# A hybrid encoder trunk on one core: step sizes of the state space mixer in three parts, two copies at high priority, a norm by token tile

## The chip, the cores and the metric

The kernel runs on one core of a Trainium2 chip. Its engines are TensorE (PE), VectorE (DVE), ScalarE (ACT), GpSimd (POOL) and SyncE (SP), which issues nearly all DMAs. The metric is the device time of one execution in microseconds, as a median over runs.

## What is computed

One layer is applied to two independent sequences, a prompt of 256 tokens and a sample of 512, with the same weights and a width of 1024. Together they are 768 tokens, six token tiles of 128.

```python
def trunk(x, ...):
    h = rmsnorm(x, norm1)
    (gq, gk, gv, gg, glr, dq, dk, dvv, sz, sxbc, sdt) = jnp.split(h @ w_in, IN_OFFSETS, axis=-1)
    o_gla  = gla_mixer(gq, gk, gv, gg, glr, ...)         # gated linear attention, 4 heads
    o_diff = diff_mixer(dq, dk, dvv, ...)                # differential attention, 4 heads
    o_ssd  = ssd_mixer(sz, sxbc, sdt, ...)               # state space mixer, 8 heads
    x = x + jnp.concatenate([o_gla, o_diff, o_ssd], axis=-1) @ w_out
    h = rmsnorm(x, norm2)
    return x + jnp.square(jax.nn.relu(h @ w_mlp1)) @ w_mlp2

def ssd_mixer(sz, sxbc, sdt, ...):
    ...
    dt_f = jax.nn.softplus(sdt[..., :8] + dtb_f)         # the step sizes, one row per head
    dt_b = jax.nn.softplus(sdt[..., 8:] + dtb_b)
    la = dt * a_neg                                      # its running sums give all decays
```

Everything is in fp32. A matrix product is made of three matmuls on halves of fp32 (high by high, low by high, high by low), so each large product costs three.

## The kernel before, in words

**Products.** A unit of weights is 1 MB. It comes in two DMAs of 512 KB into the buffers `wr`; ACT casts each to the high half `wh` (L133), DVE subtracts for the low half `wl` (L134). There are two buffers each of `wr`, `wh` and `wl`. `fm_unit` makes outputs with features on the partitions (tiles `fm`), `tm_unit` with tokens on them (tiles `tm`: 48 matmuls of 256 columns for two token tiles), `tok_product` adds products with `w_out` and the second MLP weights to the residual `xres` (tiles `tp`). The three tiles `fm`, `tm` and `tp` share a pool of three PSUM banks with the transposes `xT` of the second norm of the prompt; all else in PSUM (gates, `tms`, `kTp`, `U`, attention products and so on) shares the other five.

**Gated linear attention.** Two head pairs, hp 0 and 1. `gla_gates` computes running sums of the gates for each: a small product `gate` (L275), ACT and DVE work, a scan. `gla_qk` makes q and k with four `fm` tiles, which ACT copies to SBUF (L304). `gla_core` prepares `qst` and `kst` on DVE, transposes `kst` (`kTp`, L358), copies it (ACT, `kT`, L359), makes the states (`U`, L368, then S), and works through seven levels: exponentials, DVE products, PE products `att` (L435), DVE merges into `A` (L436). Then comes the output `gout` (L446, L447). Here core 0 and core 1 mean the passes of `gla_core` for hp 0 and hp 1. The `tm` products of other parts are spread between the small ones of the cores as filling for PE.

**Step sizes.** `ssd_dt` works on 16 rows: ACT and DVE operations on 16x768, a scan into `dpre` (L499), two writes of the running sums to DRAM (`scr`) and one of the totals (`scp`, L511), a read of the totals back to all partitions (`ptb`, L514), their exponential `decs` on ACT (L519), 12 transposes (`tms`, `tmb`) with nine ACT copies (L528, L532) and six small operations `ew`. Its results are first used in the state space mixer, after both cores. In the code it stands ahead of the gates.

**Second norm of the prompt.** After the last product with `w_out` (`tok_product(y_op, ...)`, column half outside, tile inside), `norm_transpose` squares each tile on ACT, scales it on DVE (`xn`, L176), transposes it on PE (`xT`, L183), and evicts it twice (ACT L184, DVE L185) into `h2`. Two token tiles lie side by side in one bank, so there are eight evictions of 256 columns on each engine. The MLP starts when they are done.

**What sets the order.** The code is written per stage; a list scheduler orders each engine's instructions when the kernel is built, by priority and its own model of durations. `tc.high_priority()` raises what is issued inside it; `tc.issue_after` holds an instruction behind another. On the chip every engine then runs its list in that order, and waits on semaphores.

Of the kernel before, what the change touches and what calls it, by code (L numbers as in the profile page):

```python
# [13 lines left out]
AF = mybir.ActivationFunctionType  # L14
# [5 lines left out]
P = 128  # L20
D = 1024
# [3 lines left out]
SEQS = ((0, 2), (2, 6))  # L25
EPS = 1e-6
LAMBDA_INIT = 0.2
N_IN, N_S3, N_T3, N_T2, N_TT, N_CC, N_DL, N_RAW, N_ACC = 12, 6, 6, 4, 8, 5, 7, 2, 3
N_F = 1024
N_S2, N_DN, N_SC = 3, 4, 2  # L30
LEVELS = (64, 32, 16, 8, 4, 2, 1)
# [11 lines left out]
def hybrid_kernel(ctx, tc, io):  # L43
    nc = tc.nc
    mm, act, dve, pool = nc.tensor.matmul, nc.scalar, nc.vector, nc.gpsimd
# [22 lines left out]
    i3 = tag(ctx, "in", N_IN, 776)  # L68
# [4 lines left out]
    t3 = tag(first, "t3", N_T3, 776)  # L73
# [116 lines left out]
    for tiles in ((0,), (1,), (2, 3), (4, 5)):  # L190
        normed = norm_transpose(xt, 0, tiles, hT, lambda x: (x[:, 0:512], x[:, 512:1024], junk), mx, small, rstd1, tiles[0] * P)

    log_ins = []
# [32 lines left out]
    zdt = s3("zdt")  # L226
# [71 lines left out]
    def gla_qk(hp):  # L298
        c0 = hp * P
        q, k = i3("gq"), i3("gk")  # L300

        def keep(dst, scale):
            def consume(ps, ts):
                act.activation(dst[:, ts], ps, AF.Copy, scale=scale)  # L304
            return consume

        w = load_unit(lambda r: [(0, P, w_in[:, r, C_GQ + c0:C_GQ + c0 + P]),
                                 (P, 2 * P, w_in[:, r, C_GK + c0:C_GK + c0 + P])], (KT, 256))
        fm_unit(w, 0, P, keep(q, 0.125), halves_)
        fm_unit(w, P, P, keep(k, 1.0), halves_)  # L310
        return q, k
# [12 lines left out]
        tm_unit(w, gcons)  # L324
        return sg

    def gla_core(pre, qk, v):
        Pf, Pb = pre
        q, k = qk

# [22 lines left out]
        for h in range(2):  # L353
            kT = t3("kT")
            for (a, b) in ((0, 4), (4, 6)):
                ps = mx("kTp")
# [25 lines left out]
                                                 U(c)[64:128, :], op0=ALU.mult, op1=ALU.add)  # L382
            S.append(sv)

        A = [c4("A", n=T) for _ in range(2)]
# [9 lines left out]
        for li, s in enumerate(LEVELS):  # L397
# [31 lines left out]
            for (a, b) in ((0, 4), (4, 6)):  # L429
                for h in range(2):  # L430
                    hs = slice(64 * h, 64 * h + 64)
                    ps = mx("att")
# [8 lines left out]
        for h in range(2):  # L441
            for (a, b) in ((0, 4), (4, 6)):
                ps = mx("gout")
# [32 lines left out]

    def ssd_dt():

        ps_ = slice(96, 112)
        z, t1, u, l = zdt[ps_], t3("dz")[ps_], t3("dt2")[ps_], t3("dl")[ps_]  # L480
        act.activation(t1, z, AF.Abs)
        act.activation(t1, t1, AF.Exp, scale=-1.0)
        act.activation(l, t1, AF.Ln, bias=1.0)
        dve.tensor_scalar(u, t1, 1.0, -1.0, op0=ALU.add, op1=ALU.add)
        dve.tensor_tensor(t1, t1, u, ALU.subtract)
        act.activation(u, l, AF.Exp, scale=-1.0)
        dve.tensor_tensor(t1, t1, u, ALU.mult)
        dve.tensor_tensor(l, l, t1, ALU.add)
        stk = t3("stk")
        pool.memset(stk, 0.0)  # L490
        dve.scalar_tensor_tensor(stk[0:16], z, 0.0, l, op0=ALU.max, op1=ALU.add)
        dtl = t3("dtl", n=W129)
        lv_ = v129(dtl[ps_])
        pool.memset(lv_[:, :, 0:1], 0.0)

        dve.tensor_scalar(lv_[:, :, 1:129], v128(stk[0:16]), sdtc[0:16, 3:4], -128.0, op0=ALU.mult, op1=ALU.max)
        pre = t3("dpre", n=W129)
        pr = v129(pre)[ps_]
        dve.tensor_tensor_scan(pre[ps_], resetm[ps_], dtl[ps_], 0.0, ALU.mult, ALU.add)  # L499
        act.copy(v128(stk[32:48]), pr[:, :, 1:129])  # L500
        act.copy(v128(stk[64:80]), pr[:, :, 0:128])
        tot = bc(pr[:, :, 128:129], [16, NT, P])
        dve.tensor_tensor(v128(stk[96:112]), tot, pr[:, :, 1:129], ALU.subtract)
        stb = t3("stb")
        dve.tensor_tensor(v128(stb[0:16]), tot, pr[:, :, 0:128], ALU.subtract)

        scr = dram.tile([16, T], F32, name="scr")
        scp = dram.tile([16, NT], F32, name="scp")
        nc.sync.dma_start(out=scr[0:8, :].rearrange("h (c i) -> h c i", i=P), in_=pr[0:8, :, 1:129])
        nc.sync.dma_start(out=scr[8:16, :].rearrange("h (c i) -> h c i", i=P), in_=pr[8:16, :, 0:128])  # L510
        nc.sync.dma_start(out=scp, in_=pr[:, :, 128])  # L511

        ptb = const.tile([P, 2, 8, NT], F32, name="ptb")
        nc.sync.dma_start(out=ptb.rearrange("p d h c -> p (d h c)"),  # L514
                            in_=bc(scp.rearrange("h c -> (h c)")[None, :], [P, 16 * NT]))
        decs = const.tile([P, NT, 2, 4], F32, name="decs")
        for g in range(2):
            gs = slice(64 * g, 64 * g + 64)
            act.activation(decs[gs], ptb[gs, :, 4 * g:4 * g + 4, :].rearrange("p d h c -> p c d h"), AF.Exp)  # L519

        tms = const.tile([P, NT, 40], F32, name="tms")
        tmb = const.tile([P, NT, 16], F32, name="tmb")
        for (a, b) in ((0, 4), (4, 6)):
            ps = mx("tms")
            for c in range(a, b):
                nc.tensor.transpose(ps[:, (c - a) * P:(c - a) * P + 112], stk[0:112, c * P:(c + 1) * P], ident[0:112, 0:112])
            for o, r, n in ((0, 0, 16), (16, 32, 8), (24, 72, 8), (32, 96, 8)):
                act.copy(tms[:, a:b, o:o + n], v128(ps)[:, :b - a, r:r + n])  # L528
        ps = mx("tmb")
        for c in range(NT):  # L530
            nc.tensor.transpose(ps[:, 16 * c:16 * c + 16], stb[0:16, c * P:(c + 1) * P], ident[0:16, 0:16])
        act.copy(tmb, ps[:, :96].rearrange("p (c r) -> p c r", c=NT))  # L532
        ew = const.tile([P, NT, 2, 2, 8], F32, name="ew")
        act.activation(ew[:, :, 0, 0, :], tms[:, :, 16:24], AF.Exp)
        act.activation(ew[:, :, 0, 1, :], tmb[:, :, 8:16], AF.Exp)
        act.activation(ew[:, :, 1, 0, :], tms[:, :, 32:40], AF.Exp)
        act.activation(ew[:, :, 1, 1, :], tms[:, :, 24:32], AF.Exp)
        dve.tensor_tensor(ew[:, :, 1, 0, :], ew[:, :, 1, 0, :], tms[:, :, 0:8], ALU.mult)
        dve.tensor_tensor(ew[:, :, 1, 1, :], ew[:, :, 1, 1, :], tms[:, :, 8:16], ALU.mult)
        return scr, decs, tms, ew  # L540

    def ssd_conv(us, xt, bcm):
        def conv(j):
# [310 lines left out]
    w_out = io["w_out"][0].rearrange("(k p) c -> p k c", p=P)  # L854
# [89 lines left out]
    v = gla_v(0)  # L944
# [60 lines left out]
    qg8 = const.tile([P, 1], F32, name="qg8")  # L1005
    dve.tensor_scalar(qg8, col(R_QN), 0.125, None, op0=ALU.mult)

    dt = ssd_dt()
    pre = [gla_gates(hp) for hp in range(2)]

    masks = t2("masks").bitcast(U8)[:, :len(LEVELS) * P].rearrange("p (l i) -> p l i", i=P)
    for a, b in ((0, 4), (4, 7)):
# [34 lines left out]
    dve.tensor_scalar(nlam, nlam, -LAMBDA_INIT, None, op0=ALU.add)  # L1047

    qk = gla_qk(0)
    core = gla_core(pre[0], qk, v)  # L1050
    qk, v = gla_qk(1), gla_v(1)
    sg = gla_gate_out(0)
    gla_out(0, core, sg)
    core = gla_core(pre[1], qk, v)
    sg = gla_gate_out(1)
    gla_out(1, core, sg)

# [4 lines left out]
    dl = tag(second, "dl", N_DL, 512)  # L1062
# [64 lines left out]
    def norm2(tiles, h2, c0, ps_of):  # L1127
        return norm_transpose(xres, 8, tiles, h2, xn_of, ps_of, small2, rstd1, c0)

    prompt, sample = (0, 1), (2, 3, 4, 5)  # L1130
# [9 lines left out]
        load_x(t, xp_)  # L1140
    tok_product(from_column(gla_p, 0), 4, w_out, 0, prompt)
    tok_product(from_column(mix_operands(mixa[0], range(4), u_new, dn), 0), 4, w_out, 4, prompt)
    tok_product(y_op, 4, w_out, 8, prompt)
    h2p = [both_in(hp_)("h2", 256) for _ in range(KT)]
    normed = [z.ins for z in norm2(prompt, h2p, 0, acc)]

    for f in range(0, 4096, N_F):
        mlp(f, N_F, [(h2p, 0, 256, 0)], prompt, u_new, dn, store if f == 4096 - N_F else None, (scaled, normed) if f == 0 else ())
# [53 lines left out]
```

## Time and profile before

| | |
|---|---|
| median of 3 runs | 1186.19 us (1180.62 to 1189.1) |
| profiled execution | 1190.88 us, of which the span of the trace is 1188.8 us |
| mean granted TensorE clock | 0.978 |
| busy: PE / DVE / ACT / POOL | 96% / 65% / 46% / 14% |

A profile is of one execution. A busy share is a mean over stages: up to about 460 us the mixers run, up to about 830 us the products with `w_out`, the rest of the attention and the prompt's MLP, and after that the sample's MLP. Idle time is printed in front of the instruction that ended it, with the instruction or DMA that released it. The granted clock is 1.0 where the throttle let TensorE run at 2.4 GHz, and 0.5 where it ran at 1.2 GHz.

### The profile page before, as it was taken

To read this page: it belongs to the slowest core of one execution; us is meant where nothing else is said; L and a number is where in the kernel's file an instruction comes from. 1 tells how busy PE (TensorE), PEld (TensorE's weight loads), DVE (VectorE), ACT (ScalarE), POOL (GpSimd) and SP (SyncE) were. 2 spreads that over 40 slices of the span, in tenths; PEclk is the share of its full clock that TensorE was granted. 3 is DMA by queue.
4 is the path that set the end of the run, shared out by engine and by line. 5 is a ranking of instruction groups with operands and counts; after the bars stand their busy time and mean duration, and the time that the engine had idled before them with its cause. 6 is when DMAs were issued, how large, how long until landed. Compare 5 with 4: busy or idle time off the path is not lost.

```text
span 1188.8 us, 17623 instructions
## 1 busy us (share of the span) xinstructions
PE 1136.2 (96%) x6788; PEld 999.4 (84%) x6788; DVE 768.7 (65%) x1366; ACT 541.1 (46%) x1037; POOL 162.8 (14%) x207
## 2 busy tenths in 40 slices
PE   7979999999999998899988999999999999999998
PEld 7979899899998887698878897787987788787786
DVE  6558979775479577896786687766544444444443
ACT  7455345256266426665765673435322322322331
POOL 2003324140310262110100002200000000000000
PEclk9989999799999999899999999999999999999999
DMA  6312021143254346245645457642232232232331
GB/s 193 96 39 69 4 63 37 36 155 119 65 172 113 109 149 203 74 142 185 186 131 171 134 164 236 228 150 72 72 106 92 86 106 87 91 107 79 99 106 71
DMA packets 118856, 136.62 MB, mean 115 GB/s; under 512 B 8951, under 2 KB 86901, under 8 KB 118773
## 3 DMA queue, kind: packets, MB, share of 16 engines
q1 hardware_dynamic: 118741, 135.50, 36.7%
q8 instruction: 53, 0.87, 0.3%
q14 instruction: 30, 0.25, 0.1%
q10 hardware_dynamic: 32, 0.01, 0.0%
HBM read 121.80 MB, written 13.68 MB: 114 GB/s over the span
## 4 chain that ended last, share of the span: by engine, by line
PE 41%; DMA 12%; DVE 9%; ACT 6%; issue 2%; POOL 0%; SPq 0%; ACTq 0%; DVEq 0%; POOLq 0%
DMA wr<-in_w_mlp 8%; PE tp L97 7%; PE tp L98 7%; PE tp L99 7%; PE fm L97 5%; PE fm L98 5%; PE fm L99 5%; DVE wl L134 3%; ACT wh L133 3%; DMA wr<-in_w_out 2%; DMA er<-scr 1%; DVE zh L558 1%; DVE xres L877 1%; PE tm L97 1%; PE tm L99 1%
## 5 line engine op out<-in xcount | busy, mean ns | idle before, releaser
L133 ACT CAST wh<-wr 128x1024 fp32r<-128x1024 f32 x186 | 189.2, 1048 | 250.5 <-PE tp L99 128.2
L134 DVE TENSOR_TENSOR wl<-wr,wh 128x1024 fp32r<-128x1024 f32 x186 | 228.8, 1252 | 107.7 <-ACT wh L133 105.8
L99 PE MATMUL tm<-wh,hTl 128*128 128x256 f32 x576 | 169.8, 295 | 0.0
L97 PE MATMUL tm<-wh,hTh 128*128 128x256 f32 x576 | 168.0, 292 | 1.7 <-ACT xp L552 1.6
L98 PE MATMUL tm<-wl,hTh 128*128 128x256 f32 x576 | 168.2, 292 | 0.0
L877 DVE TENSOR_TENSOR xres<-tp,xres 128x512 f32<-128x512 f32 x116 | 77.7, 686 | 98.3 <-PE tp L99 98.0
L97 PEld LDWEIGHTS tm<-wh,hTh 128*128 128x128 f32 x576 | 112.3, 195 | 4.0 <-ACT xp L552 1.8
L98 PEld LDWEIGHTS tm<-wl,hTh 128*128 128x128 f32 x576 | 112.1, 195 | 1.7 <-DVE wl L134 0.2
L99 PEld LDWEIGHTS tm<-wh,hTl 128*128 128x128 f32 x576 | 112.2, 195 | 1.3
L98 PE MATMUL fm<-h2l,wh 128*128 128x512 f32 (+1 forms) x288 | 107.1, 373 | 0.0
L97 PE MATMUL fm<-h2h,wh 128*128 128x512 f32 (+1 forms) x288 | 106.9, 373 | 0.0
L99 PE MATMUL fm<-h2h,wl 128*128 128x512 f32 (+1 forms) x288 | 106.7, 371 | 0.0
L97 PE MATMUL tp<-wh,uh 128*128 128x512 f32 x256 | 101.5, 396 | 0.6
L98 PE MATMUL tp<-wl,uh 128*128 128x512 f32 x256 | 100.5, 392 | 0.0
L99 PE MATMUL tp<-wh,ul 128*128 128x512 f32 x256 | 99.7, 395 | 0.0
L97 PE MATMUL fm<-h,wh 128*128 128x256 f32 x256 | 72.3, 284 | 2.4 <-ACT relu L923 2.1
L98 PE MATMUL fm<-h,wh 128*128 128x256 f32 x256 | 72.2, 283 | 0.0
L99 PE MATMUL fm<-h,wl 128*128 128x256 f32 x256 | 71.5, 283 | 0.6 <-DVE wl L134 0.6
L923 ACT ACTIVATE relu<-fm 128x256 f32<-128x256 f32 (+1 forms) x68 | 31.6, 468 | 70.3 <-PE fm L99 70.3
L97 PEld LDWEIGHTS fm<-h2h,wh 128*128 128x128 f32 x288 | 54.7, 190 | 10.1
L99 PEld LDWEIGHTS fm<-h2h,wl 128*128 128x128 f32 x288 | 54.6, 190 | 10.0
L98 PEld LDWEIGHTS fm<-h2l,wh 128*128 128x128 f32 x288 | 54.7, 190 | 9.9
(323 smaller groups left out, 2499.4 us busy)
## 6 DMA issues: line engine op xcount, KB each, us to landing
wr<-in_w_mlp SPq DMA_DIRECT2D x128, 512.0 KB
wr<-in_w_in SPq DMA_DIRECT2D x30, 512.0 KB
wr<-in_w_out SPq DMA_DIRECT2D x24, 512.0 KB
ar<-scr SPq DMA_DIRECT2D x6, 512.0 KB
er<-scr SPq DMA_DIRECT2D x6, 512.0 KB
x<-in_x_sample SPq DMA_DIRECT2D x4, 512.0 KB
wr<-in_w_in SPq DMA_DIRECT2D x8, 256.0 KB
xres<-in_x_sample SPq DMA_DIRECT2D x4, 512.0 KB
```

Source lines behind the costliest of these rows:

```text
L97: mm(out, lhsT=lh, rhs=rh, start=first, stop=False)
L98: mm(out, lhsT=lh, rhs=rl, start=False, stop=False)
L99: mm(out, lhsT=ll, rhs=rh, start=False, stop=last)
L133: act.copy(hi, raw)
L134: dve.tensor_tensor(lo, raw, rd(hi), ALU.subtract)
L558: dve.scalar_tensor_tensor(zh, xp[:, k:k + 772], half[:, 6 * k + j:6 * k + j + 1], zh, op0=ALU.mult, op1=ALU.add)
L877: dve.tensor_tensor(xres[t][:, cs], ps, xres[t][:, cs], ALU.add)
L923: act.activation(r, ps, AF.Relu)
```

## The change

1. `ssd_dt` becomes a generator in three parts. Part 1 (absolute value, exponential, logarithm) runs after q and k of hp 0, part 2 (the DVE and ACT work, the scan and the three writes to DRAM) after the output of core 0, part 3 (`ptb`, `decs`, transposes, `ew`) within core 1, between its states and its levels. Four tiles move between pools, and one pool grows by a buffer.
2. The copies of q and k out of PSUM are issued at high priority.
3. The last product with `w_out` of the prompt runs tile by tile, and the norm of each tile is issued at high priority as soon as its product is done, 128 columns wide: 16 evictions on each of ACT and DVE instead of eight, and the same 16 transposes.

```diff
-N_IN, N_S3, ... = 12, 6, ...
+N_IN, N_S3, ... = 12, 7, ...
@@ gla_qk
         def keep(dst, scale):
             def consume(ps, ts):
-                act.activation(dst[:, ts], ps, AF.Copy, scale=scale)
+                with tc.high_priority():
+                    act.activation(dst[:, ts], ps, AF.Copy, scale=scale)
@@ gla_core, between the states S and the levels
+        if between is not None:
+            between()
@@ ssd_dt
-        z, t1, u, l = zdt[ps_], t3("dz")[ps_], t3("dt2")[ps_], t3("dl")[ps_]
+        z, t1, l = zdt[ps_], i3("dz")[ps_], i3("dl")[ps_]
         act.activation(t1, z, AF.Abs)
         act.activation(t1, t1, AF.Exp, scale=-1.0)
-        act.activation(l, t1, AF.Ln, bias=1.0)
+        log_ins.append(act.activation(l, t1, AF.Ln, bias=1.0).ins)
+        yield
+        u = t3("dt2")[ps_]
...
         nc.sync.dma_start(out=scp, in_=pr[:, :, 128])
+        yield
 
         ptb = const.tile([P, 2, 8, NT], F32, name="ptb")
...
-        return scr, decs, tms, ew
+        yield scr, decs, tms, ew
@@ main
-    dt = ssd_dt()
     pre = [gla_gates(hp) for hp in range(2)]
+    dt_steps = ssd_dt()
...
     qk = gla_qk(0)
+    next(dt_steps)
+    dt = []
     core = gla_core(pre[0], qk, v)
     qk, v = gla_qk(1), gla_v(1)
     sg = gla_gate_out(0)
     gla_out(0, core, sg)
-    core = gla_core(pre[1], qk, v)
+    next(dt_steps)
+    core = gla_core(pre[1], qk, v, lambda: dt.extend(next(dt_steps)))
...
-    tok_product(y_op, 4, w_out, 8, prompt)
     h2p = [both_in(hp_)("h2", 256) for _ in range(KT)]
-    normed = [z.ins for z in norm2(prompt, h2p, 0, acc)]
+    normed = []
+
+    def normed_tile(t, c):
+        if c == D:
+            with tc.high_priority():
+                normed[:] = [z.ins for z in norm2((t,), h2p, t * P, acc)]
+
+    tok_product(y_op, 4, w_out, 8, prompt, normed_tile, True)
```

The order of the built kernels shows it at three places. **The gates on PE.** Before, the transposes of the step sizes stand ahead of the first gates, near the end of the first `fm` of hp 1 (its last matmul but one):

```order
L98 MATMUL fm_1319<-hTl_135,wh_1307 128x384
L526 MATMUL tms_682<-ident,stk_657 128x112 x4
L526 MATMUL tms_691<-ident,stk_657 128x112 x2
L531 MATMUL tmb_698<-ident,stb_668 128x16 x6
L275 MATMUL gate_713<-rst_328,wg_534 128x512
L275 MATMUL gate_714<-rst_328,wg_534 128x256
L99 MATMUL fm_1319<-hTh_134,wl_1308 128x384
```

With the change the gates stand in the second `fm` of hp 0, three `fm` tiles (72 matmuls) earlier:

```order
L98 MATMUL fm_790<-hTl_135,wh_752 128x384
L275 MATMUL gate_646<-rst_328,wg_534 128x512
L275 MATMUL gate_647<-rst_328,wg_534 128x256
L275 MATMUL gate_662<-rst_328,wg_534 128x512
L275 MATMUL gate_663<-rst_328,wg_534 128x256
L275 MATMUL gate_678<-rst_328,wg_534 128x512
L99 MATMUL fm_790<-hTh_134,wl_753 128x384
```

All that is left of the `tms` and `tmb` transposes there has moved to core 1. **The start of core 1, on ACT and PE.** Before, ACT goes from the exponentials of core 1 to casts, a `dqk` copy and `kT`:

```order
L346 ACTIVATE kf_1815<-kf_1815 128x768
L197 ACTIVATE gg_2167<-tm_2285 128x256
L133 CAST wh_2612<-wr_2614 128x1024
L133 CAST wh_2612<-wr_2618 128x1024
L197 ACTIVATE gg_2168<-tm_2285 128x256
L737 COPY dqk_2466<-tm_2417 128x512
L359 COPY kT_1824<-kTp_1825 128x512
```

With the change ACT's list there is this (`gg` are the output gates of hp 1):

```order
L506 COPY stk_1741<-dpre_1747 16x768
L507 COPY stk_1741<-dpre_1747 16x768
L197 ACTIVATE gg_2167<-tm_2179 128x256
L197 ACTIVATE gg_2167<-tm_2232 128x256
L338 ACTIVATE eb_1765<-eb_1765 128x768
L347 ACTIVATE kf_1777<-kf_1777 128x768
L526 ACTIVATE decs<-ptb 64x48 x2
L197 ACTIVATE gg_2167<-tm_2285 128x256
L133 CAST wh_2612<-wr_2614 128x1024
L133 CAST wh_2612<-wr_2618 128x1024
...
L360 COPY kT_1786<-kTp_1787 128x512
```

`decs`, which needs the DMA of `ptb`, now stands ahead of the copy `kT`. PE's list at the same place, with the change:

```order
L99 MATMUL tm_2285<-wh_2169,hTl_135 128x256
L359 MATMUL kTp_1787<-ident,kst_1762 128x128 x4
L359 MATMUL kTp_1793<-ident,kst_1762 128x128 x2
L369 MATMUL U_1798<-gv_1361,kT_1786 128x128 x2
L369 MATMUL U_1805<-gv_1361,kT_1786 128x128 x4
L359 MATMUL kTp_1819<-ident,kst_1763 128x128 x4
L359 MATMUL kTp_1825<-ident,kst_1763 128x128 x2
L97 MATMUL tm_2417<-wh_2407,hTh_120 128x256
```

Before, 25 matmuls of a `tm` tile stood between the first transposes and the first U; now there are none. **The norm of the prompt, on PE.** With the change, the transposes of tile 0 (`xn_6430`, `xn_6431`) stand in front of the products of tile 1 (`tp_6472`, `tp_6486`), where before they came after all products:

```order
L636 MATMUL U_5133<-wx_5128,btm_4586 64x256 x2
L818 MATMUL sc_5147<-ks_5022,qs_5021 128x512
...
L183 MATMUL xT_6440<-ident,xn_6430 128x128
...
L819 MATMUL sc_5183<-kz_2402,qs_5056 128x512
L183 MATMUL xT_6456<-ident,xn_6431 128x128
...
L183 MATMUL xT_6468<-ident,xn_6431 128x128
L97 MATMUL tp_6472<-wh_6382,yh_4985 128x512
```

The 24 matmuls of tile 1's products follow, then its eight transposes, between the products `sc` and `wT` of the differential attention, then the MLP's first `fm`.

## Rows read from the trace of the kernel before

**Rows 1.** The page, part 1 (busy us, share of the span, instructions)
```profile
PE 1136.2 (96%) x6788; PEld 999.4 (84%) x6788; DVE 768.7 (65%) x1366; ACT 541.1 (46%) x1037; POOL 162.8 (14%) x207
```

**Rows 2.** Windows: us, busy per engine, granted clock, DMA share, GB/s
```profile
76.00:81.00 5.00, 4.92 (x15) 4.73 (x16) 2.37 (x6) 4.94 (x18) 0.00 (x0) 0.50 0.21 71
210.00:228.00 18.00, 18.00 (x81) 16.21 (x80) 15.16 (x24) 4.22 (x5) 4.25 (x2) 0.53 0.22 59
228.00:246.00 18.00, 18.00 (x161) 16.86 (x160) 10.34 (x25) 5.00 (x21) 0.00 (x0) 1.00 0.10 31
460.00:496.00 36.00, 27.95 (x136) 20.74 (x136) 31.93 (x62) 25.76 (x50) 4.60 (x7) 0.86 0.38 112
830.00:1188.00 358.00, 354.26 (x1594) 288.09 (x1592) 158.03 (x197) 99.05 (x133) 0.00 (x0) 1.00 0.29 92
```

**Rows 3.** Timeline of ACT, 54 to 76 us: start, us, instruction, idle before, releaser
```profile
54.19 0.49 ACT L304 ACTIVATE gq<-fm 128x384 f32<-128x384 f32 x1
74.96 0.58 ACT L519 ACTIVATE decs<-ptb 64x48 f32<-64x48 f32 x2 [9.20 <-DMA ptb<-scp]
75.55 0.80 ACT L528 COPY tms<-tms 128x64 f32<-128x64 f32 x8
```

**Rows 4.** Timeline of DVE and of SP's queue, the step sizes' scan and DMAs
```profile
54.20 0.95 DVE L485 TENSOR_TENSOR dz<-dz,dt 16x768 f32<-16x768 f32 x1 [0.23 <-ACT dl L483]
59.82 1.77 DVE L499 TENSOR_TENSOR_SCAN dpre<-resetm,dtl 16x774 f32<-16x774 f32 x1
63.22 0.62 SPq L511 DMA_DIRECT2D scp<-dpre  x1
69.81 0.34 SPq L514 DMA_DIRECT2D ptb<-scp  x1
```

**Rows 5.** Timeline of PE, gates, start and end of the two cores
```profile
76.08 0.79 PE L275 MATMUL gate<-rst,wg 96*128 96x512 f32 x1 [7.52 <-ACT tms L528]
103.43 0.87 PE L358 MATMUL kTp<-ident,kst 128*128 128x128 f32 x6 [0.56 <-DVE kst L350]
156.88 0.39 PE L446 MATMUL gout<-gv,A 128*128 128x128 f32 x2
177.82 0.28 PE L97 MATMUL tm<-wh,hTh 128*128 128x256 f32 x1
182.43 0.28 PE L97 MATMUL tm<-wh,hTh 128*128 128x256 f32 x1
182.55 0.82 PE L358 MATMUL kTp<-ident,kst 128*128 128x128 f32 x6
239.44 0.38 PE L446 MATMUL gout<-gv,A 128*128 128x128 f32 x2
```

**Rows 6.** DVE by lines, 188 to 240 us (count, busy, mean ns, idle before, releaser)
```profile
L436 DVE COPY_PREDICATED A<-masks,att 128x512 f32<-128x512 uint8 (+1 forms) x28 | 14.9, 580 | 7.0 <-PE att L435 6.8
L134 DVE TENSOR_TENSOR wl<-wr,wh 128x1024 fp32r<-128x1024 f32 x2 | 3.4, 1712 | 0.0
```

**Rows 7.** Timeline of DVE and ACT, the start of core 1
```profile
172.22 0.95 DVE L336 TENSOR_TENSOR eb<-pre 128x768 f32<-128x768 f32 x1
177.23 1.99 ACT L133 CAST wh<-wr 128x1024 fp32r<-128x1024 f32 x2
188.00 0.34 DVE L375 SCALAR_TENSOR_TENSOR S<-S,dec,U 64x128 f32<-64x128 f32 x1 [1.99 <-ACT S L373]
```

**Rows 8.** Timeline of DVE, ACT and PE, the norm of the prompt
```profile
479.77 0.69 DVE L877 TENSOR_TENSOR xres<-tp,xres 128x512 f32<-128x512 f32 x1
480.55 1.06 ACT L171 ACTIVATE xn<-xres 128x1024 bf16<-128x1024 f32 x1 [1.59 <-DVE xres L877]
482.66 1.15 DVE L176 TENSOR_SCALAR xn<-xres,rs 128x512 f32<-128x512 f32 x2
483.74 1.42 DVE L134 TENSOR_TENSOR wl<-wr,wh 128x1024 fp32r<-128x1024 f32 x1
488.27 1.54 PE L183 MATMUL xT<-ident,xn 128*128 128x128 f32 x6 [4.33 <-DVE h L185]
```

More of the change, by code (lines that the diff above doesn't have):

```diff
@@ L27 @@
 LAMBDA_INIT = 0.2
-N_IN, N_S3, N_T3, N_T2, N_TT, N_CC, N_DL, N_RAW, N_ACC = 12, 6, 6, 4, 8, 5, 7, 2, 3
+N_IN, N_S3, N_T3, N_T2, N_TT, N_CC, N_DL, N_RAW, N_ACC = 12, 7, 6, 4, 8, 5, 7, 2, 3
 N_F = 1024
@@ L325, in gla_gate_out, with gla_core @@
         return sg
-    def gla_core(pre, qk, v):
+    def gla_core(pre, qk, v, between=None):
         Pf, Pb = pre
@@ L488, in ssd_dt @@
         dve.tensor_tensor(l, l, t1, ALU.add)
-        stk = t3("stk")
+        stk = i3("stk")
         pool.memset(stk, 0.0)
@@ L503, in ssd_dt @@
         dve.tensor_tensor(v128(stk[96:112]), tot, pr[:, :, 1:129], ALU.subtract)
-        stb = t3("stb")
+        stb = i3("stb")
         dve.tensor_tensor(v128(stb[0:16]), tot, pr[:, :, 0:128], ALU.subtract)
```

## The prediction

> **What bounds the kernel now.** I read the page's busy times first: PE works 1136.2 of 1188.8 us [rows 1]. So the end is set by PE, and a change gains only by taking idle time or half clock from PE, or loses by adding some. The number of PE matmuls is the same in both kernels, so I compare PE's position: how far it is in its list at a given time. Then I read the windows by stage [rows 2]: from 830 us on PE is busy for 354.26 of 358 us with a clock of 1.00, and the change touches nothing there. At 76 to 81 us it is busy but at 0.50 of its clock, at 210 to 228 at 0.53, and at 460 to 496 it works only 27.95 of 36 us. Last the timelines, for what stands behind each.
>
> The first place is the step sizes. Their scan ends at 59.82 + 1.77 = 61.59 us, `scp` is issued at 63.22, `ptb` at 69.81 because SP waits for `scp` to land [rows 4], and ACT, idle for 9.20 us, gets to `decs` at 74.96 and to the `tms` copies at 75.55 [rows 3]. So scan to `decs` takes 13.4 us. The first gate waits 7.52 us for those copies [rows 5]: `tms`, `tmb` and the first two gates hold all five banks of their pool. After the wait PE runs 5 us at half clock [rows 2], which costs 2.5 us.
>
> The second place is core 1, bound by DVE and then by PE at half clock: DVE's merges waited 6.8 us for `att` [rows 6].
>
> The third is the norm of the prompt: PE waits 4.33 us for DVE's evictions, behind 2 x about 1.3 us of weight splits [rows 8].
>
> **The first gates: -10.0 us.** In the new order nothing of the step sizes stands ahead of the gates on PE, and they move up by three `fm` tiles. They need `rst`, which is ready before the copy of q at 54.19 us [rows 3], so I see no new wait. Gone are 7.52 and 2.5 us. The gates' chain to the first `kTp` took 103.43 - 76.08 = 27.35 us [rows 5]. Started at about 54 it ends at 81, while PE, with 110 fewer matmuls of filling (in units of 256 columns) at that point, breaks even at 103.43 - 110 x 0.118 = 90.4. The unit is (182.43 - 177.82) / 39 steps = 0.118 us [rows 5]. So core 0 starts at least 9 us ahead. It is bound by DVE and keeps its 53.4 us [rows 5] or a little less. I take PE to be 10 us ahead at the end of core 0, so `gout` of core 0, which stands 127 units earlier in the list, starts at 156.88 - 15.0 - 10 = 131.9.
>
> **The start of core 1: the wait comes back, +6 us.** The three DMAs and `decs` now follow core 0. Before, DVE began core 1 (`eb`) 172.22 - 156.88 = 15.3 us after the start of `gout` [rows 5, 7]. With the change two weight splits (3.4 us [rows 6]) and the step sizes' DVE chain (54.20 to 61.59, 7.4 us [rows 4]) stand ahead, so the scan ends 26.1 us after `gout`, at 158.0. PE reaches `kTp` after the 25.7 us of before [rows 5] and 78 units more, 25.7 + 9.2 = 34.9, at 166.8. `kst` needs from `eb` on 7.6 us as before, plus `stk` and `stb` (like `eb`, 0.95 each [rows 7]) and about 0.8 for two merges, 10.3 in all: 168.3. That is a first wait of 1.5 us (up to 4 with DVE's own waits).
>
> Then U needs `kT`, and on ACT `kT` stands behind `decs`. If the way through DRAM takes 13.4 us again, `decs` starts at 171.4; then come 0.6 for itself, 1.99 for the casts [rows 7] and about 1.6 for three gates and a copy, so U starts at about 175.7. Transposed and copied without `decs` it would be about 169.7. So PE is idle for some 6 us more than the chain needs, with no filling in its list between `kTp` and the next `tm`. Behind `decs` on ACT stand those gates, casts and copies; who waits is PE.
>
> The skill's notes weigh on this from two sides. The row: 13.4 us from scan to `decs` with the DMA queues nearly empty [rows 3, 4]. The Trainium skill, "DMA: Bandwidth & Descriptors", section on the anatomy of one DMA, puts the fixed cost of a transfer at about 2 us; two of them in a row would then make about 5 us (an estimate from that page), `decs` would be long done, and this term would be 0 in place of +6. I go by the row.
>
> **Core 1 itself: 0 to -8 us, taken at 0.** Before, DVE's first S at 188.00 to `gout` at 239.44 took 51.4 us [rows 5, 7], of which 3.4 were splits that now stand earlier and 6.8 waits for `att` [rows 6]. So 41.2 to 48 us. S comes 1.8 us after U, at 177.5, and `gout` at 218.7 to 225.5. PE then stands 107 units earlier in its list, so it breaks even at 239.44 - 12.6 = 226.8: 1.3 to 8.1 us ahead. The `tms` transposes, copies and `ew` now lie in here, where ACT has room. How much of the 6.8 us goes depends on the clock, which at 210 to 228 was 0.53 in a stretch where PE had little filling and had waited [rows 2]; now there are 122 units of filling where there were 180. I take half, and get 4 us ahead after core 1: -10 + 6 = -4 with this term at 0.
>
> **q and k copies: 0.** Each takes 0.49 us on ACT [rows 3], and they only feed chains costed above.
>
> **The norm by tile: +4 us.** In the new order tile 0's transposes stand ahead of tile 1's products, and PE goes in order, so those products do not hide it. From the last `xres` (479.77) to `xn` done (482.66 + 1.15) were 4.0 us [rows 8]. PE has four `sc` and a few U for that time, some 1.5 us, and waits 2.5 us; the eight evictions follow, with only three banks, partly hidden by `sc` and `wT`: 2.5 more. Tile 1 has the same, with a weight split of 2 x 1.3 us ahead of its evictions, and less some filling: 6. Together 11 us, against 4.6 before (4.33 and two short waits). The clock there was 0.86, 5.0 us lost in 36 [rows 2], about 3.4 behind the long wait; I expect to get 2.4 of that back, since the waits are shorter. 11 - 4.6 - 2.4 = +4. Bounds: -1 if the chains hide half of it, +8 if the clock falls twice. The eight more evictions on each engine, 128 wide, lie inside this. Between 246 and 460 us the order moves too, by little, and I count 0, plus or minus 3.
>
> **Sum.** -10 + 6 + 0 + 0 + 4 = 0 against the profiled 1190.88 us. That run is 4.7 us above the median of 1186.19; against the median the forecast is 1186 us, no change. About 1% (12 us) is what a measurement of this kernel can tell from no change.
>
> **Rivals.**
> A, faster: the way through DRAM does not hold ACT in its new place, and core 1 runs without DVE's waits for `att`. Then the 6 us fall away and 8.1 are gained in place of 4: -10 - 4 = -14, with the norm at +4 to -1: 1172 to 1176. For it speaks that nothing in DVE's list is behind `decs`, and that 6.6 us of the way were SP's wait for a write of 96 numbers; against it, that this happened on quiet queues. It decides if `decs` comes within about 10 us of the scan. The Trainium skill's DMA page, cited above, is on its side, and the trace of before is not.
>
> B, slower: the same way gets longer. In the new order on SP the DMAs of the sums stand behind four writes of core 0's output and a 512 KB weight transfer, and the next weights follow `ptb`. Every us above 13.4 is a us of PE, since no filling stands there; at 20 us U starts at 182, PE is idle for 14 us, and core 1 goes on at half clock. Its 242 matmuls need 242 x 18 / 161 = 27 us at full and 242 x 18 / 81 = 54 at half [rows 2], more than DVE's 48, so `gout` comes at 236: 9 us behind in place of 4 ahead. With the norm: +13, or 1199. It decides from a way of about 20 us on. On the clock, the Trainium skill, "TensorE: Matmul & The Clock Gate", part 1, says that an idle array falls back to half rate; the rows after the 7.52 us wait agree (0.50).
>
> C, the norm does what it is written for: a chance that tile 0's transposes find their data ready since U and `sc` fill the time. Then +4 becomes -1, and the time 1181, still no change.
>
> **How the numbers follow.** The forecast with its bounds, C included: 0.62, 1177 to 1194. A: 0.22. B: 0.16. The range for 8 in 10 goes from 1171 to 1199. Faster by over 1%: 0.22, nearly all A. Slower by over 1%: 0.15. Within 1%: 0.63.
>
> **What the profile would show.** Right, step by step: no wait at the first gate and a clock of 1.0 there; `kTp` of core 0 at about 81 us, its `gout` at about 132; ACT idle ahead of `decs` for a wait on `ptb`, U of core 1 at about 176, its `gout` at about 222; two groups of waits at `xT`. Wrong: `decs` without idle time ahead of it (A), a way of over 20 us or a clock of about 0.5 through core 1 (B), PE without waits at tile 0's `xT` (C), or a first `kTp` much later than 85 us, for which the gates' chain would have a wait that I did not see.

## The result and the profile after

The changed kernel takes 1205.82 us (median; 1202.06 to 1208.53) against 1187.64 us before: a ratio of 1.017, with a 95% interval of 1.014 to 1.020. The forecast of no change was wrong; the kernel is slower by about 18 us. The profiled execution took 1207.41 us, 16.5 more than that of before, at a mean granted clock of 0.971.

The page's part 1 of the changed kernel (busy us, share of the span, instructions) answers to [rows 1]:

```profile
PE 1144.6 (95%) x6788; PEld 1002.8 (83%) x6788; DVE 774.9 (64%) x1374; ACT 543.0 (45%) x1045; POOL 158.2 (13%) x207
```

The number of matmuls is the same. PE is busy 8.4 us longer and idle about as much longer. The windows of the changed kernel (stretch, length, busy us and instructions of PE, PEld, DVE, ACT and POOL, granted clock, DMA share, GB/s) say where:

```profile
76.00:81.00 5.00, 5.00 (x38) 5.00 (x37) 4.88 (x5) 2.56 (x4) 0.27 (x1) 1.00 0.01 3
157.00:188.00 31.00, 22.17 (x171) 21.42 (x171) 27.45 (x41) 17.28 (x44) 12.63 (x16) 0.83 0.16 48
457.00:508.00 51.00, 36.62 (x160) 25.75 (x159) 40.14 (x80) 31.66 (x69) 4.55 (x7) 0.83 0.32 97
507.00:720.00 213.00, 206.10 (x1358) 183.11 (x1357) 165.70 (x304) 138.85 (x282) 25.25 (x23) 0.99 0.52 160
733.00:765.00 32.00, 25.50 (x89) 18.63 (x88) 19.30 (x38) 12.21 (x23) 5.95 (x9) 0.84 0.76 254
845.00:1204.00 359.00, 355.78 (x1595) 288.51 (x1594) 158.05 (x197) 99.00 (x133) 0.00 (x0) 1.00 0.28 91
```

The same places in the kernel before, each taken where about the same work stands there:

```profile
455.00:495.00 40.00, 31.95 (x149) 23.45 (x148) 33.62 (x63) 26.81 (x53) 4.60 (x7) 0.87 0.43 130
495.00:707.00 212.00, 201.47 (x1317) 179.91 (x1315) 159.79 (x285) 135.56 (x280) 17.68 (x20) 0.98 0.51 156
725.00:750.00 25.00, 22.57 (x101) 16.46 (x101) 15.56 (x29) 9.87 (x17) 4.79 (x5) 1.00 0.95 295
```

The gates now run between 51 and 58 us, at a granted clock of 1.00, and the half-clock stretch behind them is gone (0.50 in [rows 2], now 1.00). A new poor stretch stands at 157 to 188 us, where core 1 starts: PE works 22 of 31 us. The stretch with the norm grew from 40 to 51 us. A second one follows at 733 to 765: 25.50 us of PE work in 32 us at a clock of 0.84, where before it was 22.57 us in 25 at 1.00.

I then put PE's list beside its times, as the prediction did. Negative is ahead of before. At points where both kernels have done the same matmuls, the changed kernel stands at -2.7 us from 254 to 357 us, -0.3 at 440, +1.2 at 456, +14.3 at 795, +15.8 from 900 to 1000 and +16.5 at the end. Between such points the order differs, and the position is an estimate that weights each matmul by its columns: some -10 us at 84 us, +11 at 508, +6 to +8 at 720. So the gain of the gates was real; 7 of its 10 us were used up by the end of core 1, and the rest by 456 us. The loss comes in two places, one at the norm and one that the prediction did not speak of.

PE's timeline of the changed kernel (start, us, instruction, idle before and its releaser), in order of time: the gates, core 0, the start and end of core 1, the last product and the norm, and the second place:

```profile
51.39 0.87 PE L275 MATMUL gate<-rst,wg 96*128 96x512 f32 x4
78.77 0.82 PE L359 MATMUL kTp<-ident,kst 128*128 128x128 f32 x6
131.59 0.38 PE L449 MATMUL gout<-gv,A 128*128 128x128 f32 x2
171.50 1.54 PE L359 MATMUL kTp<-ident,kst 128*128 128x128 f32 x6 [4.93 <-DVE kst L351]
176.95 1.44 PE L369 MATMUL U<-gv,kT 128*128 128x128 f32 x5 [3.91 <-ACT kT L360]
224.11 0.38 PE L449 MATMUL gout<-gv,A 128*128 128x128 f32 x2
469.15 0.49 PE L97 MATMUL tp<-wh,yh 128*128 128x512 f32 x1 [1.72 <-ACT wh L133]
471.21 0.80 PE L98 MATMUL tp<-wl,yh 128*128 128x512 f32 x1 [1.57 <-DVE wl L134]
482.64 0.52 PE L183 MATMUL xT<-ident,xn 128*128 128x128 f32 x3 [2.23 <-ACT pr L821]
483.78 0.47 PE L183 MATMUL xT<-ident,xn 128*128 128x128 f32 x1 [0.63 <-DVE h L185]
488.71 0.33 PE L183 MATMUL xT<-ident,xn 128*128 128x128 f32 x1 [1.09 <-DVE h L185]
498.86 0.52 PE L183 MATMUL xT<-ident,xn 128*128 128x128 f32 x3 [2.68 <-DVE xn L176]
502.63 0.99 PE L183 MATMUL xT<-ident,xn 128*128 128x128 f32 x3 [3.26 <-DVE h L185]
506.96 0.56 PE L97 MATMUL fm<-h,wh 128*128 128x256 f32 x1
738.99 0.50 PE L97 MATMUL tp<-wh,u 128*128 128x512 f32 x1 [2.05 <-ACT wh L133]
760.30 0.79 PE L98 MATMUL tp<-wl,moh 128*128 128x512 f32 x1 [2.56 <-DVE wl L134]
```

The MLP's first `fm`, at 506.96, started at 494.00 before:

```profile
494.00 0.42 PE L97 MATMUL fm<-h,wh 128*128 128x256 f32 x1
```

SP, DVE and ACT of the changed kernel, the step sizes in their new place and ACT at the second place:

```profile
159.34 1.77 DVE L505 TENSOR_TENSOR_SCAN dpre<-resetm,dtl 16x774 f32<-16x774 f32 x1
162.72 0.61 SPq L517 DMA_DIRECT2D scp<-dpre  x1
168.99 0.34 SPq L521 DMA_DIRECT2D ptb<-scp  x1
172.86 0.58 ACT L526 ACTIVATE decs<-ptb 64x48 f32<-64x48 f32 x2 [7.70 <-DMA ptb<-scp]
176.31 0.86 ACT L360 COPY kT<-kTp 128x512 f32<-128x512 f32 x2
735.85 2.16 ACT L657 ACTIVATE er<-er,tms 128x128 f32<-128x128 f32 x7 [7.43 <-DMA er<-scr]
737.91 1.03 ACT L133 CAST wh<-wr 128x1024 fp32r<-128x1024 f32 x1
```

The first group shows that `decs`, which waits for the second of two DMAs in a row, stands ahead of `kT`, for which U waits. The last two show the same pattern: `er` (the row terms of the sample's last chunk of the state space mixer) waits 7.43 us for its DMA, and behind it is a weight cast of the prompt's MLP, for which PE waits (2.05 us at 738.99; `u` is what goes into the second MLP product).

### The profile page after: what moved, and what is told of

Its sections match the earlier page's. It is cut to its first block, busy times and chain, and to the rows that moved or that the text cites. A ratio compares the mean times of both kernels' runs of the same rounds, so it can differ in the third digit from the quotient of the medians.

```text
span 1205.3 us, 17640 instructions
## 1 busy us (share of the span) xinstructions
PE 1144.6 (95%) x6788; PEld 1002.8 (83%) x6788; DVE 774.9 (64%) x1374; ACT 543.0 (45%) x1045; POOL 158.2 (13%) x207
## 4 chain that ended last, share of the span: by engine, by line
PE 61%; DVE 16%; DMA 12%; ACT 6%; issue 3%; POOL 2%; SPq 0%; ACTq 0%; DVEq 0%; POOLq 0%
DMA wr<-in_w_mlp 8%; PE tp L97 7%; PE tp L98 7%; PE tp L99 7%; PE fm L97 7%; PE fm L99 6%; PE fm L98 6%; DVE wl L134 5%; PE tm L99 5%; PE tm L97 5%; PE tm L98 5%; ACT wh L133 2%; PE att L438 2%; DVE xres L884 1%; DVE zh L565 1%
```

## The experiments

Each ratio is against the kernel before on the same chip, with its 95% interval. All of these kernels compute everything.

### Which part loses

**The old norm in the changed kernel.** The products go by column again, and the norm follows whole.

```diff
+    tok_product(y_op, 4, w_out, 8, prompt)
-    normed = []
-    def normed_tile(t, c): ...
-    tok_product(y_op, 4, w_out, 8, prompt, normed_tile, True)
+    normed = [z.ins for z in norm2(prompt, h2p, 0, acc)]
```

> The changed kernel with the last product with w_out and the norm of the prompt as before (whole columns, both tiles, 256 wide); steps sizes in three parts and q/k priority stay. Theory N (the norm by tile costs the time: PE lost some 11 us around it and 4 more in the stage that follows, while the mixers come out even at 240 us): 1186 to 1190 us, 0.999 to 1.003 of before, waits at xT as before (4 to 5 us), the gates' wait gone and 9 us of waits at kTp and U of core 1. Theory D (the parted step sizes cost it, by half clock and a different order behind core 1): 1200 to 1206 us.

Measured: 1190.69 us, 1.0025 (1.0005 to 1.0044). The MLP's first `fm` starts at 493.4 us. So the norm by tile costs some 16 us, and parts 1 and 2 of the change together cost some 3 (0.6 to 5 by the interval) in place of the -4 forecast.

**The norm alone in the kernel before** (the same edit the other way round).

> The kernel before with only the norm by tile (third part of the change). Theory N: 1198 to 1206 us, with waits for the second weight unit (tp after 12 matmuls), at xT of tile 0 and of tile 1, clock 0.5 twice, and the gates' wait of 7.5 us still there. Theory D: 1186 to 1190.

Measured: 1200.83 us, 1.0114 (1.0073 to 1.0154). The gate's wait is still there (8.16 us), and the long waits of `xT` are close to those of the changed kernel: 1.85, 2.40 and 3.26 us against 2.23, 2.68 and 3.26. `fm` starts at 507.5.

**The copies of q and k alone in the kernel before.**

```diff
-                act.activation(dst[:, ts], ps, AF.Copy, scale=scale)
+                with tc.high_priority():
+                    act.activation(dst[:, ts], ps, AF.Copy, scale=scale)
```

> The kernel before with only the copies of q and k at high priority. Both theories: no change, 1186 to 1190 us; the first gate still waits some 7 us for the tms copies.

Measured: 1189.19 us, 1.0003 (0.9979 to 1.0028): nothing, as the prediction had it.

### What in the norm costs it

**Products by tile, the norm whole behind them.** This keeps the new order of the weights and undoes the rest.

```diff
-    tok_product(y_op, 4, w_out, 8, prompt, normed_tile, True)
+    tok_product(y_op, 4, w_out, 8, prompt, None, True)
+    normed = [z.ins for z in norm2(prompt, h2p, 0, acc)]
```

> The changed kernel with the products by tile, but one norm of both tiles at the end, 256 wide, at ordinary priority. Weights as the cost: 1192 to 1196, waits at tp for wh and wl of 3 us and half clock there, one wait at xT as before. The norm in pieces as the cost: 1187 to 1190, with tp waits that something else hides.

Measured: 1191.92 us, 1.0035 (1.0010 to 1.0060). PE still waits 1.67 us for `wh`, and `fm` starts at 495.4. So tile order brings forward the second unit of weights, and this costs some 2 us at the place. In the time it is 1 us, which is inside the two intervals.

**Products by tile, both 128-wide pieces behind all of them.**

```diff
+    tok_product(y_op, 4, w_out, 8, prompt, None, True)
+    for t in prompt:
+        normed[:] = [z.ins for z in norm2((t,), h2p, t * P, acc)]
```

> The changed kernel with products by tile and the norm in two pieces of 128 columns, 16 evictions on each engine, but both pieces written after all products (in the change, tile 0's piece is written ahead of tile 1's products; the shared banks go round in the order of the code). Theory place (two chains in series, one per tile, each with PE waiting for xn and for the evictions, because tile 0's transposes stand ahead of tile 1's products): one long wait as before and a few us for eight more evictions per engine: first MLP product at 496 to 500 us, 1189 to 1195. Theory pieces (the narrow evictions are the cost wherever they stand): 503 to 507 and 1200 to 1206.

Measured: 1190.75 us, 1.0064 (1.0038 to 1.0090). PE has one long wait at `xT`, and shorter ones of 0.52 to 1.03 us behind it. The window of the norm stands below the wait, and that of the first experiment's kernel below that:

```profile
489.20 0.99 PE L183 MATMUL xT<-ident,xn 128*128 128x128 f32 x3 [6.08 <-DVE h L185]
457.00:503.00 46.00, 33.96 (x154) 24.37 (x153) 38.52 (x75) 30.19 (x63) 4.48 (x7) 0.81 0.33 102
457.00:495.00 38.00, 30.86 (x148) 22.33 (x148) 33.06 (x60) 27.45 (x52) 4.49 (x7) 0.87 0.44 134
```

Tile order and narrow pieces together cost 8 us at the place (`fm` at 501.6 in place of 493.4). By the ratios, 1.0064 against 1.0025, half of it is won back later; in the profiled run all of it is. The change adds two things to this kernel: tile 0's piece stands ahead of tile 1's products, and both pieces have high priority. With them `fm` is at 507.0 and the ratio 1.017. So at the place more than half of the loss is there without them, and in the time they make most of it. The runs do not separate place from priority.

**The pieces where the change puts them, products by column.**

```diff
-    tok_product(y_op, 4, w_out, 8, prompt, normed_tile, True)
+    tok_product(y_op, 4, w_out, 8, prompt, normed_tile)
```

> The changed kernel, but the last product runs by columns again (both tiles for one weight unit, then the other), and each tile's norm still starts at high priority when its last product is done. Only the order of the products is undone. If the weights are the cost (a unit is used up after 12 matmuls of 0.233 us, 2.8 us, where the next takes longer to come and be split: waits of 1.7 and 1.6 us and 6.8 us at half clock), some 6 us come back: 1197 to 1200. If tile 0's norm ahead of tile 1's products is the cost, it comes back here too, in part, since only 12 matmuls of tile 1 are left to stand behind it: 1192 to 1196. If neither, 1204 to 1207.

Measured: 1204.31 us, 1.0143 (1.0111 to 1.0175), `fm` at 503.8. The order of the weights is not the main cause: the interval overlaps that of the changed kernel. PE has two rounds of waits again, with a clock that is no lower than before:

```profile
482.14 0.52 PE L183 MATMUL xT<-ident,xn 128*128 128x128 f32 x3 [2.98 <-DVE xn L176]
495.64 0.52 PE L183 MATMUL xT<-ident,xn 128*128 128x128 f32 x3 [2.68 <-DVE xn L176]
499.42 0.99 PE L183 MATMUL xT<-ident,xn 128*128 128x128 f32 x3 [3.26 <-DVE h L185]
457.00:505.00 48.00, 34.02 (x162) 24.22 (x161) 40.09 (x81) 31.86 (x70) 4.55 (x7) 0.89 0.34 101
```

**Tile 0's piece later**, behind the first half of tile 1's products.

```diff
-        if c == D:
+        if t == 1:
             with tc.high_priority():
+                t = c // 512 - 1
```

> The changed kernel with tile 0's piece of the norm written after the first column half of tile 1 and tile 1's after the second, so that 12 matmuls of 0.233 us (2.8 us) of products stand between the end of tile 0's sums and its transposes. Theory place: tile 0's wait for xn (2.2 us) goes and some of its half clock, tile 1's stays: 1198 to 1202. Theory pieces: 1203 to 1207.

Measured: 1204.24 us, 1.0177 (1.0140 to 1.0214). The expectation missed. In the built order most of tile 0's second half moved behind tile 1's first half as well, so its sums ended just ahead of its transposes and a wait of 3.06 us for `xn` stayed. The run does not show what a covered tile 0 would bring.

**Tile 0's transposes from the pool of five banks**, so that they need not take turns with the sums of the products.

```diff
-                normed[:] = [z.ins for z in norm2((t,), h2p, t * P, acc)]
+                normed[:] = [z.ins for z in norm2((t,), h2p, t * P, mx)]
```

> The changed kernel, but the transposes xT of the prompt's norm take their banks from the pool of five and not from the pool of three that the products tp use. All else stays: products by tile, the norm in two pieces, high priority, 16 evictions on each engine. Theory bank (tile 0's eight transposes come between the products of tile 0 and tile 1 only because the banks of the shared pool go round in the order of the code, so that tile 1's products wait behind the whole norm of tile 0): the products of tile 1 stand ahead of all transposes, one wait instead of two, the MLP's first fm at 495 to 499 us instead of 507.0, time 1189 to 1197. Theory pieces (narrow pieces and twice the evictions cost it): 503 to 508 us there, 1202 to 1207 in all.

Measured: 1345.0 us, 1.1321 (1.1269 to 1.1372). A miss: tile 1's products do stand ahead of all transposes now, but in that pool the transposes went behind the sample's whole attention. `fm` starts at 691.6, and the attention runs with nothing to fill it. The waits of PE between 470 and 720 us (total, count, longest):

```profile
PE wT L827 <- DVE pr L824: 57.5, 14, 8.1
```

**`er` held behind the weight casts, the rest as in the changed kernel.** The last chunk's code stands behind the prompt's MLP.

```diff
+            with tc.issue_after(hold[0]) if hold else ExitStack():
                 act.activation(er[:, h], er[:, h], AF.Identity, ...)
@@ sample's mixer
-        for c in range(2, NT):
+        for c in range(2, NT - 1):
+        last_chunk.append(ssd_chunk(NT - 1, ...))
@@ behind the MLP of the prompt
+    hold[:] = last_cast
+    for _ in last_chunk[0]:
+        pass
```

> The changed kernel with one edit: the code of the sample's last chunk of the state space mixer stands behind the MLP of the prompt, and its scalings `er` are held on ACT behind the last weight cast of that MLP. Lists of all engines are those of the changed kernel up to about 730 us. The theory is that the loss of the changed kernel has two places: the norm at 457 to 508 us, and 733 to 765 us, where ACT waits 7.43 us for the DMA of `er` with two weight casts behind it. If so, the first part stays (MLP's first fm at about 507, PE some 5 us behind before at 700), the second goes: PE's product with moh starts at 745 to 749 instead of 755.5, the window 733 to 765 has a clock above 0.95, and the time is 1195 to 1199, some 8 us below the changed kernel's 1205.8. The rival is that the second place only shows what was late from the norm, and that some other thing is late next there (weights that come late by DMA): then PE waits for wh or wl all the same, moh starts at 753 or later, and the time stays at 1202 to 1207.

Measured: 1199.44 us, 1.0095 (1.0065 to 1.0124). The windows of this kernel, the norm and the second place:

```profile
457.00:508.00 51.00, 36.68 (x163) 26.14 (x162) 39.94 (x80) 32.06 (x70) 4.56 (x7) 0.83 0.29 91
733.00:765.00 32.00, 28.64 (x121) 21.51 (x120) 22.42 (x42) 13.40 (x24) 5.66 (x8) 1.00 0.78 263
```

In the norm's stretch PE's busy time is that of the changed kernel to 0.1 us (`fm` at 506.0), and the second place is whole again: PE works 28.64 us there at 1.00, the first product with `moh` (outputs of the sample's mixers, for `w_out`) starts at 748.4 in place of 755.5, and the sample's MLP 7.2 us earlier. So `er` in front of the casts costs 0.75% or some 8 us; the edit moves the rest of that chunk's code with it, and the two are not separated. What is left of the norm by tile, 1.0095 against 1.0025 without it, is some 8 us too.

### What the step sizes do

Four of these go without the norm by tile (the first experiment's kernel); the last is made from the kernel before.

**Part 3 written behind core 1's levels.**

```diff
-    core = gla_core(pre[1], qk, v, lambda: dt.extend(next(dt_steps)))
+    core = gla_core(pre[1], qk, v)
+    dt.extend(next(dt_steps))
```

> The changed kernel with the norm of the prompt as before, and with part 3 of the step sizes (ptb, decs, transposes, ew) issued after core 1's levels instead of ahead of them. Theory ptb (decs, waiting for ptb, holds the copy kT on ACT): the 3.9 us wait of U on kT is gone, the half clock behind it shorter, gout of core 1 at 216 to 221 us instead of 225.8, time 1181 to 1186. Rival (DVE's chain ahead of kTp is what lasts, ACT is only late with it): gout of core 1 at 224 to 227, time 1188 to 1192.

Measured: 1186.43 us, 1.000 (0.998 to 1.002). It did not test what it should: the built list kept `decs`, with its 8.39 us of idle time, ahead of `kT`, and U waited 4.61 us.

**`decs` held on ACT behind the copies of core 1's states.**

```diff
+            with tc.issue_after(s_ins[0]):
                 act.activation(decs[gs], ptb[gs, ...], AF.Exp)
```

> The changed kernel with the norm as before, and decs held behind core 1's copies kT and S on ACT; all DVE work and the DMAs of the step sizes stay at the start of core 1. (With part 3 merely written later, the list still had decs ahead of kT, so that run said nothing on it.) Theory ptb (decs waiting for ptb keeps kT, and so U, waiting): U comes 4 to 5 us earlier than 178.6, gout of core 1 at 219 to 223 us instead of 225.8, time 1183 to 1187. Rival (DVE's chain only): U at 177 to 179 and gout at 225 or later, 1188 to 1192.

Measured: 1186.97 us, 1.0006 (0.9976 to 1.0036). U in the first experiment's kernel and in this one:

```profile
178.59 2.93 PE L369 MATMUL U<-gv,kT 128*128 128x128 f32 x12 [4.67 <-ACT kT L360]
173.97 2.93 PE L370 MATMUL U<-gv,kT 128*128 128x128 f32 x12 [0.29 <-ACT kT L361]
```

Core 1's `gout` starts at 220.7 in place of 225.8. So `decs` ahead of `kT` costs 5 us there. In the time, 1.0006 against 1.0025 is inside the two intervals.

**Parts 2 and 3 behind core 1's output.**

```diff
-    next(dt_steps)
-    core = gla_core(pre[1], qk, v, lambda: dt.extend(next(dt_steps)))
+    core = gla_core(pre[1], qk, v)
...
+    next(dt_steps)
+    dt.extend(next(dt_steps))
```

> The changed kernel with the norm of the prompt as before, and with parts 2 and 3 of the step sizes both after core 1 and its output. Nothing of them stands in core 1's way. Theory ptb plus chain: both waits at the start of core 1 (4.9 us at kTp, 3.9 us at U) go, PE keeps the 10 us that it is ahead after the first gates: gout of core 1 at 212 to 217 us, time 1177 to 1182. Rival (core 1 is bound by DVE and gives the lead back, whatever stands ahead of it): 1186 to 1190.

Measured: 1199.52 us, 1.011 (1.008 to 1.014). Core 1 keeps the lead of 10 us: U at 166.9, `gout` at 213.1. Then it goes. PE of this kernel, and the window behind core 1:

```profile
225.85 3.27 PE L471 MATMUL goT<-ident,o 128*128 128x128 f32 x12 [5.26 <-DVE o L466]
238.34 1.38 PE L533 MATMUL tms<-ident,stk 112*128 112x112 f32 x6 [9.22 <-ACT stk L507]
224.00:246.00 22.00, 10.93 (x56) 9.53 (x57) 15.62 (x32) 9.19 (x26) 6.76 (x8) 0.54 0.21 45
```

Only the second of these waits is for the step sizes. The first is for core 1's output `o`, and the built list has changed there too: PE has no `tm` product between 213 and 240 us here, where the first experiment's kernel has 114 between 226 and 246.

**Part 2 there, part 3 just ahead of its first use.**

```diff
-    next(dt_steps)
-    core = gla_core(pre[1], qk, v, lambda: dt.extend(next(dt_steps)))
+    core = gla_core(pre[1], qk, v)
@@ behind core 1's output
+    next(dt_steps)
@@ ahead of the first use
+    dt.extend(next(dt_steps))
```

> The changed kernel with the norm as before, part 2 of the step sizes after core 1's output, and part 3 just before its results are first used, so that the transposes stand some 1000 matmuls behind the scan. Theory (the round trip costs nothing when PE has filling between scan and transposes; with both parts directly behind core 1 it came back there, 9.2 us of waiting for the copies into stk and half clock from 223 to 245 us): gout of core 1 at 212 to 214, no wait at tms, the lead of some 10 us kept: 1175 to 1180, faster than both kernels. Rival (the order behind core 1 gives the lead away in any case): 1186 to 1198.

Measured: 1198.48 us, 1.0125 (1.0095 to 1.0156). The `tms` transposes no longer wait there, and ACT's copies do it instead:

```profile
237.21 0.83 ACT L506 COPY stk<-dpre 16x768 f32<-16x768 f32 x1 [5.52 <-DVE dpre L505]
239.53 0.58 PE L97 MATMUL tm<-wh,hTh 128*128 128x256 f32 x1 [9.81 <-ACT dqk L744]
```

Behind `stk` on ACT are the copies that free PE's banks. In both places behind core 1 an engine that meets the chain of the step sizes waits for it; the 5.25 us in front of it, for `o`, are here too.

**The kernel before, with `decs` alone moved**: still in its code order, but held on ACT behind the copies of core 0's states.

```diff
-        for g in range(2):
-            act.activation(decs[gs], ptb[gs, ...], AF.Exp)
+        def late():
+            for g in range(2):
+                with tc.issue_after(s_ins[0]):
+                    act.activation(decs[gs], ptb[gs, ...], AF.Exp)
...
     core = gla_core(pre[0], qk, v)
+    decs_late()
```

> The kernel before, with one edit: decs (the exponential that needs ptb's DMA) is held on ACT behind the S copies of core 0, so that the tms and tmb copies and the first gates do not stand behind it. Step sizes stay where they were, in one piece; norm and q/k copies as before. Theory (the wait of 7.5 us and the 2.5 us at half clock behind it are worth their length, and no work has to go elsewhere for it): first gate at 68 to 70 us instead of 76.1, gout of core 1 at 229 to 233 instead of 239.4, time 1176 to 1180. Rival (DVE's chain through the two cores, or half clock later, takes it back): 1184 to 1188.

Measured: 1177.47 us, 0.9909 (0.9876 to 0.9943): faster than both kernels. ACT, and the window around the first gates:

```profile
65.11 0.77 ACT L532 COPY tms<-tms 128x64 f32<-128x64 f32 x8
114.53 0.58 ACT L523 ACTIVATE decs<-ptb 64x48 f32<-64x48 f32 x2
60.00:80.00 20.00, 20.00 (x125) 19.62 (x124) 17.23 (x22) 18.33 (x40) 3.96 (x13) 1.00 0.18 59
```

The `tms` copies come 10.4 us earlier than in [rows 3], the gate's wait of 7.52 us [rows 5] is gone, and `decs` has its data when its turn comes. Core 0's first `kTp` starts at 92.8, its `gout` at 145.7, core 1's at 228.2: 10 to 11 us ahead of [rows 5] each, and nothing is given back.

## Why the prediction was wrong, step by step

**The gates, -10: right.** All gates run from 51.39 us without a wait at full clock (before, two gate matmuls ran at 64.99 us, and it was the third that waited 7.52 us); `kTp` of core 0 came at 78.8 (forecast 81) and its `gout` at 131.6 (131.9).

**The start of core 1, +6: right in kind, a little low.** The scan ended at 161.1 us (158.0), the trip to `decs` took 11.75 us (13.4), `decs` came at 172.9 (171.4), U at 177.0 (175.7). The first wait, for `kst`, was 4.93 us where I had 1.5 and at most 4. With `decs` held, U came 4.6 us earlier: the wait on the way through DRAM is shown as the cause. Rival A is out. It rested on the Trainium skill, "DMA: Bandwidth & Descriptors", the section on the anatomy of one DMA, by whose fixed cost of about 2 us I estimated 5 us for the two transfers. That section is on transfers issued by GpSimd, and these are issued by SP; the trace has 6.27 us from one issue to the next and 3.87 from there to `decs`. B's long way did not come either: the next weights were issued 7.2 us behind `ptb`, at 176.21, and not right behind it.

**Core 1, 0: nearly right.** `gout` came at 224.1 (222), ahead of the break-even of 226.8 by 2.7; by PE's position too the lead was 2.7 and not 4, and 0.3 at 440 us. In the time, parts 1 and 2 without the norm by tile stand at some +3 us, 7 worse than the -4 of the sum. The change puts the step sizes into a place where they cost most of what they had cost before.

**The norm, +4: the step that failed.** The idle time was right in sum: PE was idle for 51 - 36.62 = 14.4 us in the stretch and for 40 - 31.95 = 8.1 before, 6.3 more, and the forecast had 11 - 4.6 = 6.4. Part of that is luck. The waits at `xT` were sized well, 2.23 + 0.63 + 1.09 = 3.95 us for tile 0 (forecast 5) and 2.68 + 3.26 = 5.94 for tile 1 (6). But with products by tile the second unit of weights is needed after 12 matmuls, and PE waits 1.72 and 1.57 us for it, which I did not have; waits of 1.3 us for weights and 1.81 us at `yT` in the stretch before, which I did not count either, made up for most of it.

What failed is the clock. I expected to "get 2.4 of that back" since "the waits are shorter". Instead the stretch lost (1 - 0.83) x 51 = 8.7 us to the clock, where it had lost (1 - 0.87) x 40 = 5.2. So the term is 6.3 + 3.5 = 10 us in place of +4, above the bound of +8 too. The granted clock was 0.62 from 469 to 478 us behind the waits for weights, 0.66 from 483 to 488 behind tile 0's waits and 0.57 from 500 to 508 behind tile 1's. With products by column, where the waits for weights are gone and those at `xT` stay, the loss is (1 - 0.89) x 48 = 5.3 us as before: the shorter waits at `xT` gave nothing back, and the 3.5 us more stand behind the weights. The Trainium skill, "TensorE: Matmul & The Clock Gate", part 1, says that idling drops the array to half rate; the rows agree on the direction (0.50 behind 7.52 us [rows 2, 5], 0.62 behind 1.72 and 1.57), and the forecast had given the shorter waits too little of it.

**What I did not price at all: 495 to 830 us.** The prompt's MLP wins back some 4 to 6 us: PE was idle for 212 - 201.47 = 10.5 us there before and for 213 - 206.10 = 6.9 after, and the clock gave 0.99 in place of 0.98. Part of it is work that PE did earlier, while it was held up in the norm. Then 733 to 765 us loses 6.5 idle and 0.16 x 32 = 5.1 to the clock, 11.6 against 2.4 before. That the order of `er` and the casts on ACT makes it is shown by the run that holds `er` and its chunk back. Why the built order differs there when the norm is changed 250 us earlier stays open. `er` waits 5.4 to 7.4 us ahead of two of those casts in five kernels whose norm is in pieces of 128 columns (the change, the norm alone, products by column, tile 0 later, both pieces behind all products), and stands behind them with a wait of 1.3 us before and in the two with the whole norm. The order alone does not set the price: with both pieces behind all products `er` waits like this,

```profile
739.46 2.45 ACT L657 ACTIVATE er<-er,tms 128x128 f32<-128x128 f32 x8 [5.71 <-DMA er<-scr]
```

and its stretch from 728 to 755 us loses 3.5 us idle and 0.13 x 27 = 3.5 to the clock, 7.0 and not 11.6.

**The sum, redone with what was measured,** by PE's position: +1.2 us where the stretch of the norm begins (forecast -4), about +10 in it (+4), -4 in the prompt's MLP (0), +7 up to 795 us (0) and +2 from there to the end: the 16.5 us between the two profiled runs. The last 2 I did not place.

## What to carry to other kernels

An instruction that waits for a DMA can cost what stands behind it in its engine's list. So before a chain is moved away from such a wait, look for the one instruction that waits and move that alone: here two small activations held back gave 0.9%, and the chain moved in three parts gave nothing in any of the places that I tried. Work that is cut into pieces and put between products meets an engine that goes in order: ask for each piece what fills the time until its input is ready, and do not count on shorter waits to give clock back. And when such an edit changes the built order elsewhere, look there too: about half of what the norm by tile cost stood 250 us later.

## What was not expected of the hardware

The way of 96 numbers through DRAM and back took 11.75 us from the end of the scan to the first use in its new place, and 13.4 in the old one. Little of it is moving data. In the new place the DMA engines were busy for a share of 0.14 from 162.5 to 164.5 us, when the two writes of the running sums and that of the totals went through, and 0.00 from there to 171; SP issued the read at 168.99, and the share was 0.09 from 171 to 172.9. Before it was the same: 0.19 from 63 to 65 us, and 0.00 from there to 72.

And the clock does not go by the longest wait: waits of 0.2 to 3.3 us held PE at a mean granted clock of 0.83 over 51 us, against 0.87 over 40 us before, where the longest were 4.33 and 1.81, and 0.81 over 46 us in the kernel with one wait of 6.08.
